# A load of single words that nobody reads: one word of every fourth row of w1 instead of one of every row

## Chip, cores, metric

One core of a Trainium2 chip runs the program. The metric is the device time of an execution in microseconds (us), lower is better. Runs made in one batch ran on one chip, but the batches ran on different chips. A profile adds the span from the first to the last recorded instruction, which is about 1.8 us shorter than the time.

## Reference

```python
batch, seq, dim, hidden = 16, 256, 512, 2048       # x: 16x256x512, w1: 512x4096, w2: 2048x512, all float32
h = x @ w1
gate, value = np.split(h, 2, axis=-1)
h = np.maximum(gate, 0) * value
return (h @ w2).astype(np.float32)
```

w1 has 512 rows of 4096 words: 16 KB a row, 8 MB in all.

## The kernel before

The kernel keeps TensorE busy with fp16 matmuls (in a Strassen-like scheme, which does not matter here). What matters is how it gets going. SyncE's queue (q1 in the profile) loads two halves of the first block of x (tile `g_S`), then "slabs" of w1 (tile `g`). TensorE transposes x, ScalarE and VectorE cast the first slab to fp16, and then the first real matmul can start (line L255). ScalarE's queue (q10) issues one odd load before all that: `first`, one 4-byte word from each of w1's rows. No instruction reads `first`.

```python
w1_v = w1.rearrange("(e p) (g j) -> p e g j", p=P, g=2)
# ... [cut]
first = wpool.tile([P, 4], F32, name="first")                       # L171
nc.scalar.dma_start(out=first[:128], in_=w1_v[:128, :, 0, 0])       # L172: the thin load
# ... [cut]
def fetch_wl(jb, g_, n=1):                                          # a slab of w1: 128 partitions x 4 rows x n*128 words
    c, i = place[jb]
    nc.sync.dma_start(out=wl[c][:, :, g_, i * P:(i + n) * P], in_=w1_v[:, :, g_, jb * P:(jb + n) * P])   # L404
# ... [cut]
for b in (0, 2):
    nc.sync.dma_start(out=xf[:, b:b + 2], in_=x_v[0, :, b:b + 2])   # L418: "x1" and "x2" below, 512 KB each
fetch_wl(0, 0, 2)                                                   # the first slab, 512 KB
fetch_wl(0, 1, 2)
nc.sync.dma_start(out=xg[:, :2], in_=x_v[0, :, NB:NB + 2])
fetch_wl(2, 0)
fetch_wl(2, 1)
# ... [cut]
idle(NWARM)                        # warm-up matmuls without data
turn_pair(xo, 0, psw, "W")         # transposes of x1
cast_w(0, 0)                       # first slab to fp16, L400
idle(NFILL)
turn_pair(xo, 2, psx, "X")         # transposes of x2
whole[0].gates((0,))               # the first real matmul, L255
```

Row 128e+p of w1 goes to partition p, both in the thin load and in the slabs.

## Time and profile before

| | before |
|---|---|
| time, median of the first 3 runs | 309.58 us (309.32 to 309.92) |
| span of the profiled run | 307.4 us |
| TensorE busy | 300.1 us, 98% |
| first real matmul starts at | 8.44 us |
| the thin load: packets, landing after its issue | 528, 4.3 us |

The busy time of each engine, from the page of the kernel before:

```profile
span 307.4 us, 5116 instructions
...
PE 300.1 (98%) x1868; PEld 182.1 (59%) x1868; DVE 219.3 (71%) x346; ACT 189.7 (62%) x457; POOL 139.7 (45%) x127
```

The same in stretches. The first columns are the stretch and its length, then busy microseconds and number of instructions of each engine, granted clock, mean busy share of the DMA engines and GB/s:

```profile
0.00:8.44 8.44, 5.78 (x25) 2.81 (x26) 1.42 (x4) 2.33 (x4) 1.14 (x8) 1.00 0.70 237
8.44:20.00 11.56, 11.56 (x92) 8.08 (x93) 9.32 (x21) 5.75 (x14) 8.91 (x11) 1.00 1.26 262
20.00:300.00 280.00, 279.86 (x1730) 168.83 (x1728) 207.69 (x321) 180.82 (x438) 129.61 (x108) 1.00 0.40 91
```

TensorE has no gap worth naming from 8.44 us on. What can move is the head. The chain of waits of the head (start, duration, what):

```profile
0.85 0.47 SPq L418
...
1.38 0.53 SPq L418
...
1.95 6.00 DMA g<-in_w_dram
...
7.98 0.41 ACT wr L400
...
8.44 1.10 PE X L255 x8
```

So the start of the first real matmul hangs on the landing of the first w1 slab at 7.96 us. The thin load in the view of its tile; there is no line after "who waited for it":

```profile
L172 ACTq DMA_DIRECT2D first<-in_w_dram x1: 478/478/478, 0.8 to 0.8; - x1
...
who waited for it (us, times):
...
DMA to landing us min/median/max: 4.3/4.3/4.3
```

And the DMA view of the window from 1.9 to 9.9 us, which prints 40 slices of 0.2 us: the busy share in tenths, the GB/s, and then each queue's packets, MB and share:

```profile
DMA  1240017999999999999999999999999999999999
GB/s 2 12 94 0 0 51 277 390 380 380 390 380 370 410 410 410 410 410 394 354 389 353 364 353 333 348 338 364 348 343 353 358 338 348 415 338 369 389 379 399
...
q1 hardware_dynamic: 1819, 2.55, 90.0%
q10 hardware_dynamic: 528, 0.00, 3.6%
```

Three things are to be read here. At first almost nothing but the thin load's tiny packets runs (2 to 94 GB/s up to 2.5 us). Then hardly anything flows for 0.4 us (the two zeros next to each other, 2.5 to 2.9 us); this is "the pause" below. From about 3.1 us the engines are full. The slabs of w1 begin at 5.69 us, slice 19.

### The profile page before, as it was taken

Reading aid. Unit: us, or ns where it says so; the run is one execution under the profiler, and the core shown is the slowest. Engines: PE = TensorE matmul, PEld = TensorE weight load, DVE = VectorE, ACT = ScalarE, POOL = GpSimd, SP = SyncE. Lnnn points to the kernel's source line nnn. Section 1 sums busy time; section 2 is a strip of 40 time slices with the busy share of each in tenths; the row PEclk is TensorE's granted clock in tenths of the full one; section 3 lists DMA queues with packets and bytes.
Section 4 is the critical chain, followed back from the end, with each engine's and each line's share of the span. In section 5 each row is a group of like instructions: output and inputs, shape, how many; then the busy total and the mean of one; then the engine's idle time right before and its main releaser. Section 6 shows DMA issues by size and latency. Waiting matters only on the chain.

```text
span 307.4 us, 5116 instructions
## 1 busy us (share of the span) xinstructions
PE 300.1 (98%) x1868; PEld 182.1 (59%) x1868; DVE 219.3 (71%) x346; ACT 189.7 (62%) x457; POOL 139.7 (45%) x127
## 2 busy tenths in 40 slices
PE   7999999999999999999999999999999999999994
PEld 3574444588844444488864444458884444448883
DVE  1798898896468888884338888885526888888401
ACT  2557776568576676737856767656857767673230
POOL 1749999810004438980002345994000433898000
PEclk9999999999999999999999999999999999999998
DMA  6999986989614740064130010037321100000223
GB/s 226 305 205 205 209 208 184 188 152 189 236 59 102 140 102 1 2 131 144 68 139 19 16 34 2 0 69 140 138 82 57 34 6 30 0 2 0 70 87 124
DMA packets 34410, 31.54 MB, mean 103 GB/s; under 512 B 14448, under 2 KB 28784, under 8 KB 34160
## 3 DMA queue, kind: packets, MB, share of 16 engines
q1 hardware_dynamic: 24608, 20.32, 21.9%
q0 software_dynamic: 9104, 10.75, 21.2%
q8 instruction: 15, 0.25, 0.3%
q10 hardware_dynamic: 672, 0.13, 0.2%
q14 instruction: 11, 0.09, 0.1%
HBM read 24.12 MB, written 11.53 MB: 116 GB/s over the span
## 4 chain that ended last, share of the span: by engine, by line
PE 95%; DMA 2%; ACT 0%; SPq 0%; issue 0%; ACTq 0%
PE Y L205 26%; PE X L205 17%; PE W L205 17%; PE Y L291 14%; PE X L291 9%; PE W L291 9%; DMA g<-in_w_dram 2%; PE W L255 2%; PE X L255 1%; PE Y L255 1%; SPq L418 0%; PE X L390 0%; ACT Y L212 0%; ACT wr L400 0%; ACT pv L333 0%
## 5 line engine op out<-in xcount | busy, mean ns | idle before, releaser
L280 POOL TENSOR_TENSOR g_S<-g 128x512 f16<-128x512 f16 (+1 forms) x46 | 58.1, 1290 | 126.3 <-DVE g L244 126.3
L205 PEld LDWEIGHTS <-wt 128*128 128x128 f16 x488 | 47.7, 98 | 55.8 <-issue 0.3
L205 PE MATMUL X<-x_A,wr 128*128 128x512 f16 x244 | 72.5, 379 | 0.1
L205 PE MATMUL Y<-x_S,wt 128*128 128x512 f16 x244 | 72.6, 379 | 0.0
L205 PEld LDWEIGHTS <-wr 128*128 128x128 f16 x366 | 35.8, 98 | 41.4 <-issue 0.4
L232 DVE SCALAR_TENSOR_TENSOR cc<-W,pu 128x512 f32<-128x512 f32 x61 | 42.2, 692 | 24.1 <-ACT pu L226 24.0
L212 ACT COPY Y<-X 128x512 f32<-128x512 f32 x61 | 34.8, 570 | 38.0 <-PE X L205 37.6
L291 PEld LDWEIGHTS <-g_S 128*128 128x128 f16 x512 | 50.0, 98 | 5.8
L238 DVE SCALAR_TENSOR_TENSOR cc<-Y,pu 128x512 f32<-128x512 f32 x61 | 42.2, 691 | 6.3
L226 ACT ACTIVATE pu<-Y 128x512 f32<-128x512 f32 x61 | 36.4, 596 | 13.9 <-PE Y L205 13.9
L233 DVE SCALAR_TENSOR_TENSOR g<-X,cc 128x512 f16<-128x512 f32 x61 | 42.2, 692 | 2.4
L244 DVE SCALAR_TENSOR_TENSOR g<-Y,cc 128x512 f16<-128x512 f32 x61 | 41.6, 682 | 1.8 <-PE Y L205 1.8
L291 PEld LDWEIGHTS <-g 128*128 128x128 f16 x384 | 37.6, 98 | 8.2
L219 ACT ACTIVATE pu<-W 128x512 f32<-128x512 f32 x61 | 36.8, 603 | 0.3 <-PE W L205 0.3
L205 PE MATMUL W<-x_S,wr 128*128 128x512 f16 x122 | 36.3, 379 | 0.0
L205 PE MATMUL Y<-x_A,wt 128*128 128x512 f16 x122 | 36.3, 379 | 0.0
L205 PE MATMUL W<-x_S,wt 128*128 128x512 f16 x122 | 36.3, 379 | 0.0
L291 PE MATMUL X<-w,g 128*128 128x256 f16 x256 | 31.2, 273 | 0.0
L291 PE MATMUL Y<-v,g_S 128*128 128x256 f16 x256 | 30.6, 273 | 0.0
L321 DVE SCALAR_TENSOR_TENSOR o<-W,pv 128x256 f32<-128x256 f32 x16 | 6.8, 425 | 29.6 <-PE W L291 29.6
L280 POOL TENSOR_TENSOR g_S<-g,g_S 128x512 f16<-128x512 f16 x18 | 21.8, 1209 | 1.4
L280 POOL TENSOR_TENSOR g_S<-g_S,g 128x512 f16<-128x512 f16 x18 | 20.8, 1155 | 1.4
(76 smaller groups left out, 284.5 us busy)
## 6 DMA issues: line engine op xcount, KB each, us to landing
out_dram<-pv SPq DMA_DIRECT2D x15, 256.0 KB, 2.0
out_dram<-o SPq DMA_DIRECT2D x13, 256.0 KB, 2.1
x<-in_x_dram POOLq DMA_DIRECT2D x3, 1024.0 KB, 9.2
xn<-x SPq DMA_DIRECT2D x12, 256.0 KB, 3.1
g_S<-in_x_dram SPq DMA_DIRECT2D x4, 512.0 KB, 6.4
wr<-in_w_dram POOLq DMA_DIRECT2D x4, 512.0 KB, 13.0
w<-in_w_dram POOLq DMA_DIRECT2D x4, 512.0 KB, 15.3
g<-in_w_dram SPq DMA_DIRECT2D x2, 512.0 KB, 6.5
```

Source lines behind the costliest of these rows:

```text
L205: nc.tensor.matmul(ps, W(wn, self.jb)[:, b], self.xo[xn][:, b, :], start=fresh and b == 0, stop=b == 1, skip_group_check=True)
L212: nc.scalar.copy(out=self.Y, in_=self.X)
L219: nc.scalar.activation(self.p5, self.W, COPY, scale=GS)
L226: nc.scalar.activation(self.u2, self.Y, COPY, scale=-GS)
L232: nc.vector.scalar_tensor_tensor(out=self.c12, in0=self.W, scalar=GS, in1=self.u2, op0=MULT, op1=ADD)
L233: nc.vector.scalar_tensor_tensor(out=self.g[:, self.jb, :TH], in0=self.X, scalar=0.0, in1=self.c12, op0=MAX, op1=MULT)
L238: nc.vector.scalar_tensor_tensor(out=self.c22, in0=self.Y, scalar=-GS, in1=self.p5, op0=MULT, op1=ADD)
L244: nc.vector.scalar_tensor_tensor(out=self.g[:, self.jb, TH:], in0=self.Y, scalar=0.0, in1=self.c22, op0=MAX, op1=MULT)
L255: nc.tensor.matmul(ps[:, ts], W(names[e // 2], self.jb)[:, e % 2], self.a[:, e, ts], start=e == 0, stop=e == 3, skip_group_check=True)
L280: eng.tensor_tensor(go[n][:, h0:h1], go[i0][:, h0:h1], go[i1][:, h0:h1], op=op)
L291: nc.tensor.matmul(ps, go[gn][:, k, b * P:(b + 1) * P], V[vn][:, k, :], start=fresh and k == 0, stop=k == NHC - 1, skip_group_check=True)
L321: nc.vector.scalar_tensor_tensor(out=d["o1"][:, HALF:], in0=d["W"], scalar=1 / GS, in1=d["pu"][:, 1], op0=MULT, op1=ADD)
```

## The change

The thin load takes 128 words instead of 512: from every fourth row, onto 32 partitions. If the early touch of w1 has a use that needs only one word in 64 KB, the change keeps the use and pays a quarter of the price.

```diff
-    first = wpool.tile([P, 4], F32, name="first")
-    nc.scalar.dma_start(out=first[:128], in_=w1_v[:128, :, 0, 0])
+    first = wpool.tile([P // 4, 4], F32, name="first")
+    nc.scalar.dma_start(out=first, in_=w1[:, 0].rearrange("(e p k) -> k p e", e=4, k=4)[0])
```

Partition q now gets rows 128e+4q, e = 0 to 3. The order of the instructions on every engine is the same; only the shape of this one load differs.

## The prediction

> **What bounds the kernel now.** TensorE: the page gives it 300.1 us busy of a 307.4 us span, the stretch table 279.86 of the 280 us from 20 to 300 us. The chain of waits has PE in unbroken succession from 8.44 us on, so only the head (0 to 8.44 us) and the tail can move. The head in the chain: SyncE issues two x loads (0.85 to 1.91 us), then "DMA g<-in_w_dram" 1.95 to 7.95 us (first w1 slab), its cast on ScalarE 0.41 us, first real matmul at 8.44 us.
>
> **What the edited load does.** The view of the tile `first` shows no reader: nobody waits for these 4-byte words of w1, issued on ScalarE at 0.82 us, landed 4.3 us later. Its intent can only be a side effect, such as touching w1 before the big w1 loads. Its price is DMA-engine time: 512 words plus 16 completion writes = 528 packets on q10. In the packet records each takes 9 ns, 4.59 us in sum, 0.29 us for each of the 16 engines. About 250 run at 1.9 to 2.5 us, before x flows; then nearly everything pauses to 3.0 us; some 270 run between 2.7 and 4.6 us, interleaved with x's packets. There q1 moves 72 to 76 KB per 200 ns, against 80 KB once q10 is empty: the engines are full from about 3.1 us to past the first w1 landing.
>
> The Trainium skill ("DMA: Bandwidth & Descriptors", section "Queues, rings and completion order") says that each engine takes turns between its queue rows packet by packet; this trace agrees, with those 270 q10 packets spread among q1's.
>
> **What the change does.** 128 words in place of 512, about 144 packets, 8 words an engine. Each engine had run some 16 words before the pause, so all of it should be over by about 2.5 us. Instruction order on every engine is unchanged. Estimate from the packet times: 270 x 9 ns / 16 = 0.15 us less in the full stretch, upper bound (528-144) x 9 ns / 16 = 0.22 us. The q1 loads are served in order with no free time, so x, the first w1 slab and the later slabs should land about 0.15 us earlier, the first real matmul starts near 8.3 us, and since PE never waits afterwards the whole 0.15 us reaches the end. The words still span w1 at 64 KB steps, so I expect any benefit of the early touch to stay; the trace shows no pause when q1 goes from x to w1 at 5.7 us, nor at the untouched second x load, so that benefit looks small or does not depend on every row.
>
> Predicted: 309.4 us (0.05% under 309.58), 8 times in 10 between 308.8 and 310.0; the range is mostly the spread of runs. Chance of faster by over 2%: 0.005; within 2%: 0.99; slower by over 2%: 0.005.
>
> **What would show each step.** q10 packets 672 -> 288 in the queue table; `first` landing earlier than 4.8 us; no q10 packet after 3.1 us; x landing near 5.1 us (5.27 now), first w1 slab near 7.8 us (7.96 now), first w1 matmul near 8.3 us; PE busy unchanged.
>
> **What would make it wrong.** (1) The pause of all queues at 2.5 to 3.0 us is caused by `first`'s reads (then up to 0.5 us more is won). (2) Untouched rows, or another assignment of 32 partitions to engines, make the big w1 loads start cold: a pause in q1 near 5.7 us, loss up to about 0.5 us, like the pause at 2.5 us. (3) A later load, not the DMA head, limits PE, so the early landing becomes a wait. None comes near 2%.

## The result

| | before | after |
|---|---|---|
| time, median of 4 runs | 309.45 us (309.32 to 309.92) | 309.67 us (309.51 to 309.89) |
| ratio | | 1.0005, 95% interval 0.9988 to 1.0022 |
| span of the profiled run | 307.4 us | 307.8 us |
| first real matmul starts at | 8.44 us | 8.70 us |

A ratio here is the mean time of one kernel's runs over that of the other's of the same rounds, so it is not quite the ratio of the medians. The first matmul starts 0.26 us later, where the prediction had it 0.15 us earlier. The page and the stretches of the changed kernel:

```profile
span 307.8 us, 5116 instructions
...
PE 300.2 (98%) x1868; PEld 182.0 (59%) x1868; DVE 219.4 (71%) x346; ACT 189.8 (62%) x457; POOL 139.9 (45%) x127
```

```profile
0.00:8.44 8.44, 5.87 (x25) 2.81 (x25) 1.17 (x3) 2.07 (x3) 1.15 (x8) 1.00 0.74 251
8.44:20.00 11.56, 11.30 (x90) 7.96 (x91) 9.29 (x21) 6.01 (x15) 8.91 (x11) 1.00 1.26 254
20.00:300.00 280.00, 279.86 (x1728) 168.67 (x1727) 207.90 (x322) 180.99 (x438) 129.81 (x108) 1.00 0.40 91
```

TensorE lost 0.26 us between 8.44 and 20 us and nothing after that. The chain of the head:

```profile
0.86 0.47 SPq L418
...
1.38 0.46 SPq L418
...
1.88 6.33 DMA g<-in_w_dram
...
8.24 0.41 ACT wr L400
...
8.70 1.10 PE X L255 x8
```

The chain has the same links; the slab lands at 8.21 us instead of 7.96 although it was issued 0.07 us sooner. Its thin load, and the DMA view of the same window:

```profile
L172 ACTq DMA_DIRECT2D first<-in_w_dram x1: 432/432/432, 0.8 to 0.8; - x1
...
DMA to landing us min/median/max: 2.8/2.8/2.8
```

```profile
DMA  5677889999999997877999999999999999999999
GB/s 53 184 256 276 307 318 420 379 410 410 389 430 389 410 282 200 256 225 230 251 302 374 364 333 353 338 364 338 328 364 384 389 384 394 420 399 369 415 328 364
...
q1 hardware_dynamic: 2007, 2.67, 96.1%
q10 hardware_dynamic: 133, 0.00, 0.9%
```

The pause at 2.5 us is gone: x flows from the first slices on, at 184 GB/s or more from 2.1 us. In its place there is a trough, a stretch of low rate, from 4.7 to 6.1 us (slices 15 to 21: 282, 200, 256, 225, 230, 251, 302 GB/s). It begins when the first w1 packet runs (4.74 us). The same slab, from the same addresses, by the same instruction, had no trough before. It looks as if the time has moved from the first touch by the thin load to the first touch by the slab; the experiments test this.

### A measure for the head

The Trainium skill ("DMA: Bandwidth & Descriptors", section "Why a DMA increments its semaphore by 16 and not by 1") says that each engine that takes part in a load signals the end of its own share. The traces agree: each of these loads leaves 16 completion records. A load has landed with the last of them, so the slowest engine decides. In all 14 traces the first matmul starts 0.48 us after the last record of the slab. From these records:

| run | x1 | x2 | slab | x2 - x1 | slab - x2 | the same, mean of the 16 | first matmul |
|---|---|---|---|---|---|---|---|
| before | 5.27 | 6.45 | 7.96 | 1.18 | 1.51 | 1.50 | 8.44 |
| r_before | 5.25 | 6.41 | 7.92 | 1.16 | 1.50 | 1.50 | 8.40 |
| after | 4.92 | 6.26 | 8.21 | 1.35 | 1.95 | 1.88 | 8.70 |
| r_after | 4.90 | 6.23 | 8.04 | 1.33 | 1.81 | 1.66 | 8.52 |
| e_none | 4.32 | 5.67 | 7.97 | 1.35 | 2.30 | 1.65 | 8.45 |
| e_scramble | 4.47 | 5.97 | 7.72 | 1.51 | 1.75 | 1.53 | 8.21 |
| e_w2 | 5.36 | 6.88 | 8.35 | 1.53 | 1.47 | 1.65 | 8.83 |
| e_half | 5.31 | 6.47 | 7.97 | 1.16 | 1.51 | 1.50 | 8.46 |
| e_own15 | 5.12 | 6.50 | 8.02 | 1.38 | 1.52 | 1.50 | 8.50 |
| e_wrong14 | 4.96 | 6.34 | 7.85 | 1.38 | 1.51 | 1.49 | 8.33 |
| e_far | 4.99 | 6.37 | 7.82 | 1.38 | 1.45 | 1.52 | 8.30 |
| r_far | 4.95 | 6.33 | 7.80 | 1.38 | 1.47 | 1.51 | 8.29 |
| e_near | 4.19 | 6.01 | 8.12 | 1.82 | 2.11 | 2.04 | 8.61 |
| e_near7 | 4.89 | 6.27 | 8.07 | 1.38 | 1.81 | 1.59 | 8.56 |

All in us from the start of the span. A "slab - x2" near 1.50 means that the slab was not held up; more is a late slab. That column compares the slowest shares, and the slowest share of x2 and of the slab need not be on the same engine. The column beside it is the mean of the slab's 16 records less the mean of x2's 16: it does not depend on which engine was slowest. Where the two disagree, the mean tells whether w1 was read slowly, and the last record when TensorE could start. The "deficit" below sums, over the first eight slices of 0.2 us from the first w1 packet on, what q1 moved less than 70 KB (of 1024 bytes) in each. It is 14 KB before and 145 KB after. The slowness of one kernel repeats only roughly (145 and 63 KB in the two profiles of the changed kernel), and e_none, e_scramble, e_w2, e_half, e_own15, e_wrong14, e_near and e_near7 rest on one profile each.

### The profile page after: what moved, and what is told of

It reads as the page before. It is cut to its first block, busy times and chain, and to the rows that moved or that the text cites. A ratio compares the mean times of both kernels' runs of the same rounds, so it can differ in the third digit from the quotient of the medians.

```text
span 307.8 us, 5116 instructions
## 1 busy us (share of the span) xinstructions
PE 300.2 (98%) x1868; PEld 182.0 (59%) x1868; DVE 219.4 (71%) x346; ACT 189.8 (62%) x457; POOL 139.9 (45%) x127
## 4 chain that ended last, share of the span: by engine, by line
PE 95%; DMA 2%; ACT 0%; SPq 0%; issue 0%; ACTq 0%
PE Y L205 26%; PE X L205 17%; PE W L205 17%; PE Y L291 14%; PE W L291 9%; PE X L291 9%; DMA g<-in_w_dram 2%; PE W L255 2%; PE X L255 1%; PE Y L255 1%; SPq L418 0%; PE X L390 0%; ACT Y L212 0%; ACT wr L400 0%; ACT pv L333 0%
```

## The experiments

Theory: the first reads of w1 are slow ("cold"), and whoever reads first pays. Before, the thin load paid, early, and held up x meanwhile. The change made it pay for less, so that the slab pays again. First rival: chance. Second rival: the thin load only costs packets, and the trough comes from something else, such as engines out of step (their shares of a load ending far apart). Since times of the same kernel scatter by more than 0.3 us, the traces decide, and the key points are run twice.

### r_before and r_after: both kernels again

No edit.

> The kernel before, again: shows how far a profile and a time repeat. If the traces are telling, x's first slab lands again near 5.27 us, the first w1 slab near 7.96 us, first w1 matmul near 8.44 us, all queues pause at 2.5 to 3.0 us, and q1 never falls below 65 KB per 200 ns from 4.7 to 6.0 us. Ratio 1.000 +- 0.0005. If the pause or the landings move by 0.2 us, the difference between before and after is chance.

> The changed kernel, again. Theory cold start (the thin load warms the w1 reads of each DMA engine and the change lost part of it): again x from the first microsecond without the pause, q1 at 40 to 55 KB per 200 ns from 4.7 to 6.0 us, the first w1 slab near 8.2 us, ratio 1.0005 to 1.001. Rival chance: no such trough, slab anywhere from 7.8 to 8.2 us, ratio 1.000.

The DMA views of r_before and, below it, of r_after, 1.9 to 9.9 us in slices of 0.2 us:

```profile
GB/s 2 2 1 41 41 123 267 339 410 390 349 410 370 389 420 399 420 399 399 359 404 348 379 333 338 358 354 348 328 374 353 333 343 369 394 338 389 358 410 389
```

```profile
GB/s 53 164 184 164 266 297 400 328 328 379 420 389 420 389 399 389 323 271 287 282 297 358 404 379 348 394 353 353 379 348 358 394 389 358 364 405 394 364 338 369
```

Measured: r_before has the first matmul at 8.40 us, deficit 15 KB. r_after has x1 0.35 us earlier again (4.90 against 5.25 us), a trough again (271 to 323 GB/s at 5.1 to 6.1 us, deficit 63 KB), and the first matmul 0.12 us later than r_before, half of the 0.26 us of the first pair. The trough is shallower than the 40 to 55 KB a slice (200 to 275 GB/s) that were expected, and the slab landed at 8.04 us, where 8.2 us was expected. Times: r_before 309.83 us, ratio 1.0007 (0.9992 to 1.0022) against the same kernel; r_after 309.37 us, ratio 0.9993 (0.998 to 1.0006). So the pattern of the head repeats, its size is 0.12 to 0.26 us, and the time cannot show it: the kernel before alone ranged from 309.2 to 310.45 us in its 11 runs here.

### e_none: no thin load

```diff
-    first = wpool.tile([P, 4], F32, name="first")
-    nc.scalar.dma_start(out=first[:128], in_=w1_v[:128, :, 0, 0])
```

> No thin load at all. Theory cold start: x lands earlier still or as in after (under 4.9 us), then a trough in q1 when w1 begins, at least as deep or long as in after, first w1 slab at 8.2 us or later, ratio 1.0005 to 1.003. Rival pure cost (the thin load only takes packets and time, 0.15 us or the 0.55 us pause): no trough, first w1 slab at 7.3 to 7.7 us, ratio 0.998 to 0.9995.

The DMA view of e_none, 1.9 to 9.9 us in slices of 0.2 us:

```profile
GB/s 72 92 113 164 389 389 430 389 430 359 420 399 420 399 420 364 313 297 256 210 312 348 364 364 389 369 333 358 364 379 400 415 364 420 404 384 384 353 346 338
```

Measured: x is at full rate from 2.7 us and lands 0.95 us earlier than before, at 4.32 us. Then the trough comes (313, 297, 256, 210, 312 GB/s from 5.1 to 6.1 us, deficit 83 KB). 13 of the 16 shares of the slab landed by 7.31 us, the last one at 7.97 us, 2.30 us after x2. The slab lands at the same time as with the 512 words (7.97 against 7.96 and 7.92 us), and the first matmul starts at 8.45 us. Time 309.63 us, ratio 1.0021 (0.9993 to 1.005), with one run of 312.27 us. The rival "pure cost" wanted the slab at 7.3 to 7.7 us and no trough, and falls. But the theory's own figures were missed too: it wanted the slab at 8.2 us or later and a trough at least as deep or long as in after. What holds of it is the trough and the late slab measured from x2. In this kernel the whole thin load was a trade at par: it took 0.95 us from x and saved 0.80 us at the slab (2.30 - 1.50), the rest lying in x2 - x1.

### e_scramble: all rows, other partitions

```diff
-    nc.scalar.dma_start(out=first[:128], in_=w1_v[:128, :, 0, 0])
+    nc.scalar.dma_start(out=first, in_=w1[:, 0].rearrange("(p e) -> p e", e=4))
```

> All 512 rows and 528 packets as before, but row 4p+e goes to partition p instead of row 128e+p, so most rows are touched by another DMA engine than the one that later loads them. Theory that warmth belongs to each engine: trough at the start of w1 as in after or without the load, first w1 slab at 8.2 us or later. Rival that it belongs to the rows, whoever touches them: as before, no trough, slab near 7.96 us.

Measured: slab - x2 is 1.75 us, deficit 53 KB, but the first matmul starts at 8.21 us, the earliest of all. Not what was asked: the first packet of the thin load ran at 3.58 us instead of 1.94 us, although it was issued at the same 0.82 us. It let x go first. By the mean of the 16 records w1 was hardly slow (1.53 us), by the last record it was (1.75 us). So it says nothing clean about who must touch which row. Time 309.45 us, ratio 0.9999 (0.9985 to 1.0012).

### e_w2: as many words, from w2

```diff
-    nc.scalar.dma_start(out=first[:128], in_=w1_v[:128, :, 0, 0])
+    nc.scalar.dma_start(out=first, in_=w2_v[:, ::4, 0])
```

> The same 512 words and 528 packets at the same moment, but from w2 (rows 128c+p, c = 0, 4, 8, 12), so w1 is not touched before its slabs. Theory cold w1 (the pause at 2.5 to 3.0 us is the price of the first touch of w1, and it is paid once): pause shorter or gone only if w2's denser rows are cheaper, but in any case a trough at the start of the w1 slabs (below 60 KB per 200 ns) and a slowest engine that lands the first slab 0.4 us or more after the 13th; first matmul at 8.5 us or later. Rival many tiny reads (the pause is the price of 512 small packets whatever they read, the trough of after comes only from the engines being out of step): pause as in before, no trough, first matmul near 8.44 us.

The DMA view of e_w2, same window:

```profile
GB/s 1 2 1 93 195 205 277 308 359 133 349 318 308 287 236 307 358 379 379 404 384 338 287 276 236 302 379 399 384 364 389 369 353 394 379 405 389 358 389 379
```

Measured: the price is paid (x1 at 5.36 us) and nothing is had for it. The w1 slabs begin at 5.80 us, and the trough (287, 276, 236, 302 GB/s) comes at 6.3 to 7.1 us, later than in after and e_none, as the slabs themselves do. The slab lands at 8.35 us, 0.39 us later than before; the first matmul starts at 8.83 us, the latest of all. The number expected for the slowest engine was wrong: it came 0.09 us after the 13th, not 0.4 us, since here x2's slowest engine was late already. By "slab - x2" (1.47 us) this slab is not late at all: of the 0.39 us, 0.34 us lies in x2 - x1. It is the mean of the 16 records that shows w1 to be slow, by as much as without any thin load (1.65 us in both, against 1.50 us before and in e_half on the same chip). The rate also dipped earlier, at 3.7 us (133 GB/s) and from 4.5 us (287, 236 GB/s), when no w1 packet had run yet, so not every dip here is w1's. What follows: tiny reads of another array do not make w1's first reads quick; reads of w1 do. That the trough as such belongs to w1 alone is less clear from this run. Time 310.0 us in two runs, ratio 0.9982 (0.9921 to 1.0043).

### e_half: the other end of each row

```diff
-    nc.scalar.dma_start(out=first[:128], in_=w1_v[:128, :, 0, 0])
+    nc.scalar.dma_start(out=first[:128], in_=w1_v[:128, :, 1, 0])
```

> The same load as before but the word lies 8 KB further on in each row (the value half), so the row is touched and the bytes that the first slab reads are not. If touching any part of a 16 KB row warms it: as before, no trough, spread of the engines' landings of the first slab under 0.35 us, first matmul near 8.4 us. If only nearer bytes are warmed (under 8 KB): trough below 60 KB per 200 ns, spread over 0.6 us.

Measured: as before in every column (slab - x2 1.51 us, deficit 10 KB, first matmul 8.46 us), and the 16 shares of the slab land within 0.32 us. The word may lie 8 KB from what the slab reads. Time 309.67 us.

### e_own15 and e_wrong14: 16 partitions

The skill's page (section "The descriptor swizzle") says that a 128-partition transfer is dealt to the 16 engines in groups of four partitions. From that, and from the assumption that a load to 16 partitions gives partition E to engine E, these two were made to touch, or to miss, each engine's own rows (J is 4096). No record here shows which engine ran a packet, so neither the dealing nor the assumption is checked.

```diff
-    first = wpool.tile([P, 4], F32, name="first")
-    nc.scalar.dma_start(out=first[:128], in_=w1_v[:128, :, 0, 0])
+    first = wpool.tile([16, 15], F32, name="first")                                                           # e_own15
+    nc.scalar.dma_start(out=first, in_=bass.AP(w1.tensor, 0, [[4 * J, 16], [32 * J, 15]]))
+    first = wpool.tile([16, 14], F32, name="first")                                                           # e_wrong14
+    nc.scalar.dma_start(out=first, in_=bass.AP(w1.tensor, 16 * J, [[4 * J, 16], [32 * J, 14]]))
```

> 15 words for each of 16 partitions (256 packets): one row of four, rows 4E+32t, so that if partition E is served by engine E and a 128-partition slab is dealt out in groups of 4 partitions, every 64 KB group of rows is touched by the engine that will load it (about half of the words are of no use). Theory each engine must have touched its own 64 KB groups: no trough, spread under 0.35 us, first matmul at 8.3 us or earlier. Rival every row must be touched: trough and spread as in after.

> 14 words for each of 16 partitions, shifted by 16 rows, so that on the same assumptions no engine touches a group that it loads later. Theory engines' own groups: trough and spread of over 0.6 us, first matmul at 8.45 us or later. Rival that rows or groups are warm for all once anyone touched them: the same as e_own15.

The DMA view of e_own15, same window:

```profile
GB/s 53 10 10 61 154 216 359 389 420 389 420 389 420 399 420 399 399 379 374 343 364 364 364 359 348 343 364 338 358 343 364 353 348 369 405 353 389 364 348 376
```

Measured: neither has a trough (deficits 3 and 4 KB, slab - x2 1.52 and 1.51 us). e_wrong14 even starts the first matmul sooner (8.33 against 8.50 us), because its x1 landed 0.16 us sooner. So the theory of "own 64 KB groups" falls, as far as the assumed dealing holds; its figures for e_own15 (spread under 0.35 us, first matmul at 8.3 us or earlier) were missed too. But so does the rival "every row must be touched": e_own15 touches only every fourth row, as the changed kernel does, and its slab is not late. And the engines are out of step here too (the 16 shares of the slab land over 0.85 and 0.73 us, against 0.28 us before), without a late slab, so being out of step is not enough to make a slab late. What is left is the number of words for each partition or how they are spread. Times 309.49 and 309.42 us.

### e_far and e_near: the changed kernel's 128 words, dealt out otherwise

```diff
-    first = wpool.tile([P, 4], F32, name="first")
-    nc.scalar.dma_start(out=first[:128], in_=w1_v[:128, :, 0, 0])
+    first = wpool.tile([16, 8], F32, name="first")
+    nc.scalar.dma_start(out=first, in_=bass.AP(w1.tensor, 0, [[4 * J, 16], [64 * J, 8]]))      # e_far
+    nc.scalar.dma_start(out=first, in_=bass.AP(w1.tensor, 0, [[32 * J, 16], [4 * J, 8]]))      # e_near
```

> Exactly the 128 words of the changed kernel (every fourth row of w1, 144 packets), dealt out differently: partition E of 16 gets rows 4E+64t, t = 0 to 7, so each partition's words are spread over the whole of w1 at 1 MB steps. Theory the warmth belongs to the engine and to a stretch of memory larger than 64 KB around the word: the trough at the start of the w1 slabs is gone or well under half of after's (deficit under 40 KB against 70 KB per 200 ns), first matmul 8.2 to 8.45 us. Rival the words warm w1 for all engines alike: trough as in after (deficit 65 KB or more), first matmul 8.5 us or later. Rival that fewer than some 14 words an engine are not enough: trough as in after.

> Again exactly the 128 words of the changed kernel, but partition E of 16 gets rows 32E+4t, t = 0 to 7: all its words lie in one 512 KB stretch. Theory warmth of the engine: a trough at least as deep as in after and without the load (deficit 65 KB or more), first matmul 8.5 us or later. Rival warm for all: the same as e_far.

The DMA view of e_far, same window:

```profile
GB/s 83 62 21 154 216 297 379 399 389 410 399 410 410 410 410 379 405 358 328 297 317 364 384 384 358 323 292 312 358 384 353 400 394 364 415 379 389 384 343 361
```

Measured: the same 128 words, 144 packets. In e_far the slab is not late (slab - x2 1.45 us, deficit 30 KB, lowest slice in the first 1.6 us of w1 297 GB/s) and the first matmul starts at 8.30 us. In e_near it is late by 0.6 us (2.11 us, deficit 218 KB, 8.61 us). So the same words do not always make w1 quick: how they are dealt to the partitions decides. e_far and e_near ran on the same chip. One doubt: e_near's thin load also began late, its first packet at 3.40 us, like e_scramble's. Times 309.48 and 309.53 us.

### e_near7 and r_far

```diff
-    first = wpool.tile([P, 4], F32, name="first")
-    nc.scalar.dma_start(out=first[:128], in_=w1_v[:128, :, 0, 0])
+    first = wpool.tile([16, 7], F32, name="first")
+    nc.scalar.dma_start(out=first, in_=bass.AP(w1.tensor, 0, [[32 * J, 16], [4 * J, 7]]))      # e_near7
```

r_far is e_far unchanged.

> e_near began its thin load 1.5 us later than the others (3.4 us), perhaps because its words are evenly spaced; with 7 instead of 8 words a partition (rows 32E+4t, t = 0 to 6, 128 packets) the spacing is uneven. Expected: thin load from about 1.9 us. Theory warmth of the engine: trough still there (deficit 65 KB or more against 70 KB per 200 ns in the first 1.6 us of w1), first matmul 8.5 us or later. Rival that e_near's trough came from its late start: deficit like e_far's, 30 KB or less, first matmul near 8.3 us.

> e_far again, timed. Trace: deficit under 40 KB, first matmul 8.2 to 8.4 us, that is 0.05 to 0.2 us before the kernel before and 0.2 to 0.4 us before the changed one. Time: a gain of 0.1 us of 309.4 is 0.03%, below the spread of runs, so ratio between 0.998 and 1.001 and no verdict but same.

The DMA views of e_near7 and, below it, of r_far:

```profile
GB/s 63 41 20 102 246 349 369 410 369 430 389 420 399 410 389 420 333 353 312 287 328 384 364 374 405 348 338 343 328 312 369 389 374 399 384 374 410 346 371 364
```

```profile
GB/s 52 72 21 92 164 278 400 379 420 379 440 369 451 369 451 353 435 348 369 312 343 374 379 374 369 348 333 338 374 353 374 374 374 394 343 399 399 356 379 338
```

Measured: e_near7's thin load began at 1.87 us. Its slab is late by 0.31 us (slab - x2 1.81 us, first matmul 8.56 us), as the theory had it; but its deficit is only 31 KB, as the rival had it. The mean rate hides the slowest shares: 13 shares of its slab had landed by 7.60 us, the last at 8.07 us (the mean of the 16 is 1.59 us). By the landing, which is what TensorE waits for, words gathered in one 512 KB stretch for each partition do not serve. By the deficit, much of e_near's deep trough may have come from its late start. And e_near7 lacks 16 of the 128 words. So this half of the question is not settled by it. r_far repeats e_far: slab - x2 1.47 us, deficit 9 KB, first matmul 8.29 us. e_near7 and r_far ran on one chip too. The times are 309.63 us for e_near7 and 309.53 us for r_far, ratio 0.9998 (0.9982 to 1.0014): r_far is not shown to beat either kernel, though in the trace the first matmul of e_far and r_far starts 0.10 to 0.15 us before the kernel before and 0.22 to 0.41 us before the changed one (8.30 and 8.29 against 8.44 and 8.40, 8.70 and 8.52).

## Why the prediction was right, and where its reasons were wrong

**Right: what bounds the kernel, and that the change is worth next to nothing.** 309.67 us lies in the range. That says little for the steps: the range (308.8 to 310.0 us) was mostly the spread of runs, the forecast of 309.4 us had the head gain 0.15 us, and it lost 0.26 and 0.13 us. An effect of this size of either sign would have fallen into the range, so the number was right by luck as far as the mechanism goes. From the start of the first real matmul to the last end on TensorE it is 294.44 or 294.45 us in 12 of the 14 profiles (294.16 in e_none, 294.51 in e_wrong14), so what the head gains or loses reaches TensorE's end in full, as predicted. After it comes a tail of 4.47 to 5.02 us, whose differences were not looked into (4.47 and 4.48 us in the two profiles of the kernel before, 4.61 and 4.77 us in those of the changed one, 5.02 us in e_half). The first pair of spans differs by 0.40 us: 0.26 us from the head and 0.14 us from that tail (4.47 and 4.61 us).

**Right: the packets.** q10 went from 672 to 288, the thin load's from 528 to 144, at a mean of 8.2 ns each in place of 8.7. The last q10 packet of the head ran at 3.25 us; the prediction had said that all should be over by about 2.5 us and none run after 3.1 us.

**Mis-sized: "270 x 9 ns / 16 = 0.15 us less in the full stretch".** x1 landed 0.35 us earlier in both pairs. The price of the thin load was not only its packets' time, 0.29 us for each engine, but the pause: without the load x1 landed 0.95 us earlier. The prediction listed this as its first way to be wrong, and that happened.

**Failed: "so I expect any benefit of the early touch to stay".** This step turned the sign. The prediction took "no pause when q1 goes from x to w1 at 5.7 us" for a sign that the benefit was small. It was the benefit itself: without any touch there is a trough there, and the slab is 0.80 us late. The change lost part of it. It is the prediction's second way to be wrong, near the place it named (4.7 us, where w1 now began, in place of 5.7 us).

The sum for the landing of the slab, change against before, first pair and second pair: x1 -0.35 and -0.35; x2 - x1 +0.16 and +0.17; slab - x2 +0.44 and +0.31. Together +0.26 and +0.13 us (from the unrounded records), where -0.15 us was predicted. The middle term is no new wait: x2 - x1 is 1.33 to 1.38 us in the eight runs whose thin load was over early or absent, and 1.16 to 1.18 us where some of its 512 w1 words were still running beside x1 (before, r_before, e_half). In e_scramble, e_w2 and e_near it is 1.51 to 1.82 us; why was not looked into.

**What is shown and what is not.** Shown: w1 is read slowly if it has not been touched (the mean of the 16 records is 1.65 us in e_none and e_w2, against 1.50 us), and in e_none the slab is late by it; a word 8 KB further on in the row does as well (e_half); not every row is needed, and the rows alone do not decide, since the changed kernel and e_far read the same 128 words with the same 144 packets, and the slab is late by 0.31 to 0.45 us in two runs of the one and not at all in two of the other. What differs is which words go to which partitions. The changed kernel gives each partition four words at 2 MB steps, e_far eight words at 1 MB steps. The number of partitions, the words for each, their steps and the order of the reads change together, so which of these counts is not shown. No chip is known to have traced both the changed kernel and e_far, but each key contrast was also seen within one: r_before, r_after and e_none on the first, e_half and e_w2 on the second, e_far and e_near on the third, r_far and e_near7 on the fourth.

Argued only: that each DMA engine has to touch a large enough part of w1 for itself. It fits most of the runs, but the records do not say which engine a packet ran on, and e_near7 and e_scramble (mean 1.53 us, though most rows were meant to be touched by another engine) were in part against it. Open: what it is in the memory path that makes a first read slow, and how far around a touched word the effect reaches.

## What to carry to other kernels

A load that nobody reads can still do work: before making it cheaper, find what it does by taking it away, and look at the loads after it, not only at its own packets. When one view shows no hold-up at a place, ask whether something already paid for it there. And for a load on the critical path read the landing of the slowest of its 16 shares, because a mean rate can look healthy while one engine is late.

## What the Trainium skill lacked or had wrong

- "DMA: Bandwidth & Descriptors" gives latencies and rates, but nothing on a first read of a stretch of memory being slow. Here the first w1 slab landed 2.30 us after the load ahead of it when nothing had touched w1, and 1.50 us after it when 512 single words had; the rate fell as low as 210 GB/s against 333 or more.
- The same page tells how a load is dealt to the engines (section "Why a DMA increments its semaphore by 16 and not by 1"), but it does not say that the dealing matters for later loads. The same 128 words left the slab 0.31 to 0.45 us late or not at all, by how they were dealt to partitions.
- The page puts the first byte of such a load at about 0.6 us (section "Latency and other measured facts"), without saying from when. Here the first packet of the thin load ran 1.1 us after its issue began and 0.64 us after its issue ended (0.82, 1.30 and 1.94 us), so the trace agrees if one counts from the end. It does not agree for the two kernels whose words follow each other at one even step from partition to partition: their first packets ran 1.8 and 2.1 us after the end of the issue (e_near at 3.40 us, e_scramble at 3.58 us; their issue took 0.72 and 0.65 us instead of 0.48 us). Why was not looked into.
- The page's round-robin of queues by packets (section "Queues, rings and completion order") agrees with the trace before, but that section does not foretell that a queue of tiny reads can hold up the other one: hardly anything flowed from 2.5 to 2.9 us, and x1 landed 0.95 us later than without them.
